# Gate weights loaded ahead of the expert results, their split moved among the last down products, the embedding product in eight steps, and x scaled before it is transposed

## The chip, the cores and the metric

One NeuronCore of a Trainium2 chip runs the whole program. Its engines are TensorE (PE, matrix products, with weight loads PEld), VectorE (DVE), ScalarE (ACT), GpSimd (POOL) and SyncE (SP, which here only issues DMAs); each works through its own instructions in order and they meet through semaphores. 16 DMA engines move data between HBM and the on-chip memories (SBUF, and PSUM for TensorE's results). The metric is device time in microseconds (us) of one launch, the median of the runs shown.

## The reference

Two layers over 512 tokens of width 1024, all in float32. Each layer has an attention part, then a mixture of experts, then a gated embedding ("ple"):

```python
x += (sigmoid(gate_a) * y_a + sigmoid(gate_b) * y_b) @ W_o
x += HierarchicalMoE(RMSNorm(x))     # top-1 of 4 groups, top-2 of 8 experts; 32 experts, hidden 256
x += (p[i] @ W_ple) * sigmoid(RMSNorm(x) @ W_ple_gate)
```

`p[i]` is 512 x 256, `W_ple` 256 x 1024, `W_ple_gate` 1024 x 1024. The change touches the end of the second line and the third.

## The kernel before

**The expert stage.** The 32 experts are worked in 16 pairs, plus one unit (`None`) for an expert that overflowed: 17 units, i = 0 to 16. A unit's rows are fetched by POOL (`fetch`), turned (`turn`, L1134), multiplied by the gate and up weights (`up`, L1151), put through the sigmoid (`act`) and, one round later, multiplied by the down weights (`finish` and `down`, L1163 to L1170); POOL scatters the result to `ybuf` in HBM (L1183). The weights come as 99 loads of 1 MB per layer, all on SP's queue (L1006), chunks 0 to 98 here: a pair takes four for `up` and two for `down`. `Chunks.ahead` issues a load as soon as its SBUF slot (8 KB of every partition) is not among those still to be used. `expert_slots` gives the slots: chunks 0 to 56 go around the 18 of `EXPERT_SLOTS`, the last 42 around the 14 of `LATE_SLOTS`, because slots 5, 10, 11 and 12 are wanted by the embedding. The last unit (i = 16) is special: `finish` of unit 15 runs first, and its chunks are 93 to 96 (`up`) and 97, 98 (`down`); 91 and 92 are the down weights of unit 15.

**The embedding.** In round i = 11 `p` (`praw`) and `W_ple` are loaded on SP's queue; in round 12 `ple_rows` (L1196) transposes `p` and splits it, and in rounds 12 to 15 `ple_product(t)` makes one of the four token tiles of `p @ W_ple`, two halves of 512 columns each.

**The split.** A float32 product that must be exact is made of three faster ones: `split` writes the rounded value on ACT (`hi`, L139 or L142) and the rest on DVE (`lo`, L140 or L143), and `mm3` adds hi·hi, hi·lo and lo·hi (L116 to L118). Weights of a `Stream` are split in pieces; `W_ple_gate` has four column blocks of 256, sources 1 to 4 of `ws2`, each split in 8 pieces, the gain folded in.

**The results and the gate.** When all scatters are done, SP loads `yg[t]`, the two expert results of token tile t, for t = 0 to 3 (L1248), with the gate blocks 1 and 2 behind `yg[0]` and `yg[1]`, and 3 and 4 at the end. `stored(t)` adds the two results to x on DVE (L1258), the last unit's rows come through a product with `which` (L1273, L1276), the sum of squares and its rsqrt `rs` are made on ACT (L1278 to L1281), and `turn_in` (L303) transposes the raw x (L289) and splits it into `gT`. Then the gate product: first half blocks 1 and 2, second half blocks 3 and 4, for four token tiles each (24 TensorE products of 256 columns for a tile and a block). `rs` is applied afterwards: ACT takes |p·r| (L1326), and DVE min(p·r, 0) (L1330). Block 3 is written into block 1's place, and so can be split only when all products with block 1 are done.

**What sets the order.** The Tile framework puts the instructions in a fixed order on each engine when the kernel is built, by program order where an operand is expected to be ready, and fills in later work where it is not. `tc.issue_after` holds an instruction behind another on the same engine.

Of the kernel before, what the change touches and what calls it, by code (L numbers as in the profile page):

```python
# [45 lines left out]
def expert_slots(n):  # L46


    m = n - 3 * len(LATE_SLOTS)
    return [EXPERT_SLOTS[k % len(EXPERT_SLOTS)] if k < m else LATE_SLOTS[(k - m) % len(LATE_SLOTS)] for k in range(n)]  # L50


# [9 lines left out]
def trunk(ctx: ExitStack, tc: tile.TileContext, a, out):  # L62
# [33 lines left out]
    def p_proj():  # L96
        return ps.tile([128, 512], F32, name="proj", tag="proj", bufs=2)
# [204 lines left out]

    def turn_in(xs, hT, t):  # L303
        for h, p in transposed(xs):
            split(p, hT.t[h][:, :, t * 128:(t + 1) * 128])

    class Stream:

# [2 lines left out]
        def __init__(self, srcs, raws, his=(7, 8), pieces=1, first=(), eng=nc.vector, pool=(), depth=None, quick=()):  # L311
            self.pool, self.pooled = pool, None
            self.eng = eng
            self.first = first
            self.srcs, self.raw, self.low, self.done, self.i = srcs, {}, {}, {}, 0
            self.raws, self.his, self.pieces = raws, his, pieces
            self.depth = depth or len(raws)
            self.quick = quick
            self.nsplit = 0

        def load(self, i, eng=nc.sync, parts=1):
            if i < len(self.srcs) and i not in self.raw:
# [15 lines left out]
        def split(self, i, part=None, one=None):  # L338
# [13 lines left out]
            elif i < len(self.srcs) and i not in self.done:  # L352
# [19 lines left out]
                        self.apart(self.hi, lows, self.lo)  # L372
                self.done[i] = w

        def get(self, ahead=1):
            self.i += 1
            for j in range(ahead + 1):
                self.split(self.i - 1 + j)
            return self.done[self.i - 1]
# [16 lines left out]
    for l in range(L):  # L396
        std = (128, KT, 256)
        odd[0] = l % 2 == 1
        ws1 = streams[l]
        ws2 = Stream([(a["wple"][l], (128, 2, D))] + [(a["wpg"][l, c], std, gcol[:, 1]) for c in range(4)], (10, 6, 4, 9), his=(7, 8), pieces=8, first=(5,))  # L400


        if l == 0:
# [753 lines left out]
        def down(u, sg):  # L1157

            n = len_of(u)
            ws = [we.get() for _ in sides(u)]  # L1160
            pt = p_z()
            for c in range(2):
                nc.tensor.transpose(pt[:, c * n:(c + 1) * n], sg[:, c * 128:(c + 1) * 128], ident[:n, :n])  # L1163
            hid = wk.tile([128, 2, 128], F32, name="hid", tag="hid", bufs=2)[:, :, :n]
            nc.scalar.activation(hid, pt[:, :2 * n].rearrange("p (c n) -> p c n", c=2), AF.Copy)  # L1165
            for h in range(2):
                py = p_z()[:n, :]
                for c in range(2):
                    for (_, r), w in zip(sides(u), ws):
                        halves[0] = nc.tensor.matmul(py[r:r + CAP], hid[:, c, r:r + CAP], w[:, c, h * 512:(h + 1) * 512],  # L1170
                                                     start=c == 0, stop=c == 1, tile_position=(0, r),
                                                     skip_group_check=True).ins
                yield py
            we.ahead()
# [11 lines left out]

        pp = [None, None]

        halves, whole = [None], [None]

        def ple_rows():

# [4 lines left out]
                split(p[:, :256].rearrange("p (k n) -> p k n", k=2), pT[:, :, t * 128:(t + 1) * 128])  # L1197
            ws2.get(0)

        def ple_product(t):  # L1200

            wp = ws2.done[0]
            if t % 2 == 0:
                pp[t // 2] = slot(11 + t // 2, [128, 2, D], F32, f"pp{t // 2}")
            for h in range(2):
                p = p_proj()
                with tc.issue_after(halves[0]):
                    whole[0] = mm(p, lambda k: pT[:, k, t * 128:(t + 1) * 128], lambda k: wp[:, k, h * 512:(h + 1) * 512], 2).ins
                nc.scalar.activation(pp[t // 2][:, t % 2, h * 512:(h + 1) * 512], p, AF.Copy)

        last = None
        for i, u in enumerate(units):
            if i + 2 < len(units):
                gs.append(fetch(units[i + 2]))
            if i == len(units) - 6:
                praw = slot(12, [128, NT, 256], F32, "praw")
                nc.sync.dma_start(praw, a["p"][l])
                pT = xgs.tile([128, 2, 2, 512], F32R, name="pT", tag="dhi", bufs=1)
                pT = Pair(pT[:, 0], pT[:, 1])
                ws2.load(0)  # L1220
            if i == len(units) - 5:
                ple_rows()
            if i == len(units) - 1:
                finish(*last)
                break
            if i:
                nxtT = turn(gs[i + 1][0], len_of(units[i + 1]))
            sg = up(u, curT)
            if not i:
                after()  # L1230
                spill[0] = nc.values_load(spi[0:1, 0:1], engines=(mybir.EngineType.SP,), min_val=0, max_val=NE - 1)
                nxtT = turn(gs[1][0], len_of(units[1]))
            if last:
                finish(*last)
            last, curT = (u, sg), nxtT
            if i >= len(units) - 5:
                ple_product(i - len(units) + 5)

        which = wk.tile([128, 512], F32R, name="which", tag="gT", bufs=4)
        tokens = wk.tile([128, 512], F32, name="tokens", tag="gT", bufs=4)  # L1240
# [3 lines left out]
        nc.vector.tensor_scalar(which, tokens, token, None, op0=OP.is_equal)  # L1244
        ygs = []
        for t in range(NT):
            ygs.append(slot(t, [128, 2, D], F32, "yg"))
            nc.sync.dma_start(ygs[t], ybuf.rearrange("(i t p) d -> t p i d", i=2, p=128)[t])  # L1248
            if t < 2:
                ws2.load(t + 1)  # L1250
        ws2.split(1)
        sg = up(u, curT)
        ws2.split(2)

        def stored(t):

# [3 lines left out]
        gT = Halves([15, 16, 17, 18], "gT")  # L1260
        stored(0)
        y = slot(20, [128, 2, D], F32R, "y")
        for h, py in enumerate(down(u, sg)):
            split(py, Pair(y[:, 0, h * 512:(h + 1) * 512], y[:, 1, h * 512:(h + 1) * 512]))
        ws2.load(3)
        ws2.load(4)
        for t in range(NT):
            if t:
                stored(t)
# [9 lines left out]
            r = rs[:, t:t + 1]  # L1279
            nc.scalar.activation(r, ss, AF.Ln, scale=1.0 / D, bias=epsc[:, 0:1])  # L1280
            nc.scalar.activation(r, r, AF.Exp, scale=-0.5)  # L1281
            turn_in(x[:, t], gT, t)
        work2.close()


# [12 lines left out]
        for half in range(2):  # L1298
# [8 lines left out]
            for cc, t in PAIRED:  # L1307
# [12 lines left out]
                    continue  # L1320
                c0, n = (2 * half, 512) if wide else (c, 256)
                p = banks[t] if wide else banks[t][:, cc * 256:(cc + 1) * 256]
                r = rs[:, t:t + 1]
                with tc.high_priority() if not wide else ExitStack():
                    s = wk.tile([128, 512], F32, name="ps", tag="ps", bufs=3)[:, :n]
                    nc.scalar.activation(s, p, AF.Abs, scale=r)  # L1326
                    nc.scalar.activation(s, s, AF.Exp, scale=-1.0)
                    nc.scalar.activation(s, s, AF.Ln, bias=1.0)
                    z = wk.tile([128, 512], F32, name="pz", tag="pz", bufs=3)[:, :n]
                    nc.vector.tensor_scalar(z, p, r, 0.0, op0=OP.mult, op1=OP.min)  # L1330
                    nc.vector.tensor_tensor(s, z, s, op=OP.subtract)
                    nc.scalar.activation(s, s, AF.Exp)
                    cs = slice(c0 * 256, c0 * 256 + n)
                    nc.vector.tensor_tensor(s, s, pp[t // 2][:, t % 2, cs], op=OP.mult)  # L1334
                    nc.vector.tensor_tensor(x[:, t][:, cs], x[:, t][:, cs], s, op=OP.add)  # L1335
# [91 lines left out]
```

## Time and profile before

| | us |
|---|---|
| median of 3 runs | 1549.39 (1548.62 to 1550.88) |
| the profiled execution | 1544.48 |
| its span | 1542.8 |
| PE busy | 1461.7 (95%) |
| DVE busy, ACT busy | 684.4 (44%), 665.6 (43%) |
| mean granted TensorE clock | 0.977 |

The profile is of one execution, in microseconds from the start of its span. Layer 0's expert stage lies between about 440 and 710, layer 1's between about 1200 and 1476; the gate follows each. A busy PE is not a PE at its peak: while it waits for the next piece of a weight, its products follow one another with gaps, and at the lower clock each takes longer.

### The profile page before, as it was taken

Reading aid. Unit: us, or ns where it says so; the run is one execution under the profiler, and the core shown is the slowest. Engines: PE = TensorE matmul, PEld = TensorE weight load, DVE = VectorE, ACT = ScalarE, POOL = GpSimd, SP = SyncE. Lnnn points to the kernel's source line nnn. Section 1 sums busy time; section 2 is a strip of 40 time slices with the busy share of each in tenths; the row PEclk is TensorE's granted clock in tenths of the full one; section 3 lists DMA queues with packets and bytes.
Section 4 is the critical chain, followed back from the end, with each engine's and each line's share of the span. In section 5 each row is a group of like instructions: output and inputs, shape, how many; then the busy total and the mean of one; then the engine's idle time right before and its main releaser. Section 6 shows DMA issues by size and latency. Waiting matters only on the chain. (4 is left out here: it accounts for less than half of the span.)

```text
span 1542.8 us, 21365 instructions
## 1 busy us (share of the span) xinstructions
PE 1461.7 (95%) x8308; PEld 1017.3 (66%) x8308; DVE 684.4 (44%) x1494; ACT 665.6 (43%) x1448; POOL 115.0 (7%) x113
## 2 busy tenths in 40 slices
PE   9999999999989999897999999999999999979886
PEld 7767986888963333335897688778889533324386
DVE  5453565454462111217945526654445422122196
ACT  5664456554322221325846645564533122223266
POOL 0000000000121111010210000000002112110002
PEclk9999999999999999998999999999999999999998
DMA  7200214334479999985131111252262999999731
GB/s 290 104 28 28 106 59 170 100 112 182 162 277 420 418 411 407 421 358 232 56 123 55 55 42 69 83 184 96 76 263 101 354 419 419 399 420 422 316 144 55
DMA packets 60779, 325.43 MB, mean 211 GB/s; under 512 B 11428, under 2 KB 11684, under 8 KB 28032
## 3 DMA queue, kind: packets, MB, share of 16 engines
q1 hardware_dynamic: 50272, 302.10, 49.5%
q0 software_dynamic: 9248, 17.70, 3.1%
q10 hardware_dynamic: 1152, 4.19, 0.7%
q8 instruction: 68, 1.11, 0.3%
q14 instruction: 39, 0.32, 0.1%
HBM read 312.04 MB, written 28.84 MB: 221 GB/s over the span
## 5 line engine op out<-in xcount | busy, mean ns | idle before, releaser
L1151 PE MATMUL proj<-raw,gT 128*64 128x512 f32 x1056 | 259.5, 596 | 1.4 <-DVEq L1077 1.4
L140 DVE TENSOR_TENSOR wlo<-raw,whi 128x1024 fp32r<-128x1024 f32 (+1 forms) x108 | 121.1, 1142 | 135.3 <-ACT whi L139 130.7
L1151 PEld LDWEIGHTS proj<-raw,gT 128*64 128x64 f32 x1056 | 81.3, 137 | 142.3 <-issue 139.9
L1170 PE MATMUL z<-raw,hid 128*64 128x512 f32 x528 | 155.0, 634 | 2.0 <-ACT hid L1165 1.9
L139 ACT ACTIVATE whi<-raw 128x1024 fp32r<-128x1024 f32 (+1 forms) x108 | 104.4, 989 | 89.3 <-PE proj L117 57.9
L802 POOL TENSOR_TENSOR xs<-x,gb 128x512 f32<-128x512 f32 (+2 forms) x34 | 45.6, 1341 | 982.8 <-DVE x L846 819.5
L117 PE MATMUL proj<-wlo,gTh 128*128 128x256 f32 x336 | 97.9, 291 | 4.5 <-DVE wlo L143 4.3
L147 ACT ACTIVATE sgm<-proj 128x256 f32<-128x256 f32 (+1 forms) x34 | 13.0, 383 | 204.2 <-PE proj L1151 204.2
L1170 PEld LDWEIGHTS z<-raw,hid 128*64 128x64 f32 x528 | 45.2, 144 | 82.0 <-issue 72.9
L116 PE MATMUL proj<-whi,gTh 128*128 128x256 f32 x336 | 97.6, 290 | 1.4 <-ACT gTh L139 1.4
L118 PE MATMUL proj<-whi,gTl 128*128 128x256 f32 x336 | 97.2, 289 | 0.0
L1138 DVE COPY gT<-av 128x512 f32<-128x512 f32 (+1 forms) x32 | 21.5, 671 | 149.7 <-PE proj L1151 113.8
L117 PE MATMUL proj<-hTl,whi 128*128 128x512 f32 x192 | 75.6, 394 | 0.0
L117 PE MATMUL proj<-gTl,whi 128*128 128x512 f32 x192 | 75.6, 394 | 0.0
L116 PE MATMUL proj<-gTh,whi 128*128 128x512 f32 x192 | 75.4, 393 | 0.0
L116 PE MATMUL proj<-hTh,whi 128*128 128x512 f32 x192 | 75.4, 393 | 0.0
L118 PE MATMUL proj<-hTh,wlo 128*128 128x512 f32 x192 | 75.4, 392 | 0.0
L118 PE MATMUL proj<-gTh,wlo 128*128 128x512 f32 x192 | 75.3, 392 | 0.0
L116 PE MATMUL proj<-whi,mh 128*128 128x256 f32 x256 | 74.0, 290 | 0.0
L117 PE MATMUL proj<-wlo,mh 128*128 128x256 f32 x256 | 72.9, 285 | 0.0
L118 PE MATMUL proj<-whi,ml 128*128 128x256 f32 x256 | 72.6, 284 | 0.0
L117 PEld LDWEIGHTS proj<-wlo,gTh 128*128 128x128 f32 x336 | 65.9, 196 | 5.9 <-DVE wlo L143 5.9
(341 smaller groups left out, 3287.5 us busy)
## 6 DMA issues: line engine op xcount, KB each, us to landing
raw<-in_wgu_dram SPq DMA_DIRECT2D x132, 1024.0 KB, 19.3
raw<-in_wdn_dram SPq DMA_DIRECT2D x66, 1024.0 KB, 20.0
raw<-in_win_dram SPq DMA_DIRECT2D x37, 1024.0 KB, 4.8
raw<-in_wo_dram SPq DMA_DIRECT2D x8, 1024.0 KB, 4.8
yg<-ybuf SPq DMA_DIRECT2D x8, 1024.0 KB, 11.4
raw<-in_wpg_dram SPq DMA_DIRECT2D x8, 1024.0 KB, 14.9
ybuf<-zero SPq DMA_DIRECT2D x8, 512.0 KB, 5.9
brw<-in_bra_dram SPq DMA_DIRECT2D x16, 256.0 KB, 2.7
```

The lines of the kernel that those rows point to most:

```text
L116: nc.tensor.matmul(o, lhs.hi, rhs.hi, start=start, stop=False, **kw)
L117: nc.tensor.matmul(o, lhs.hi, rhs.lo, start=False, stop=False, **kw)
L118: return nc.tensor.matmul(o, lhs.lo, rhs.hi, start=False, stop=stop, **kw)
L139: r = nc.scalar.activation(dst.hi, src, AF.Copy)
L140: split_lo[0] = eng.tensor_tensor(dst.lo, src, f(dst.hi), op=OP.subtract)
L147: nc.scalar.activation(dst, src, AF.Abs)
L802: nc.gpsimd.tensor_tensor(xs[t][:, cs], x[:, t][:, cs], gb[:, cs], op=OP.mult)
L1138: nc.vector.tensor_copy(gT[h], src)
L1151: nc.tensor.matmul(p[r:r + CAP], gT[h][:, k, r:r + CAP], w[:, k], start=h + k == 0, stop=h + k == 4, tile_position=(0, r), skip_group_chec ...
L1170: halves[0] = nc.tensor.matmul(py[r:r + CAP], hid[:, c, r:r + CAP], w[:, c, h * 512:(h + 1) * 512], start=c == 0, stop=c == 1, tile_positi ...
```

## The change

- `expert_slots`: the last 56 chunks instead of 42 use `LATE_SLOTS`, so the change of rings comes at chunk 43 instead of 57.
- `p` and `W_ple` are loaded in round 7 instead of 11, `ple_rows` is in round 8 instead of 12, and the eight halves of the product are spread over rounds 8 to 15, one each.
- Gate blocks 1 and 2 are issued ahead of `yg[0]`, block 3 ahead of `yg[2]`, block 4 after the turn of tile 1. Places: block 3 in slot 10, block 4 in slot 1 (that of `yg[1]`); block 3's high part goes to slot 9 instead of block 1's place.
- Block 1 is split in `begin` and `piece`: four pieces behind the activation that makes `hid` of the last unit, and ahead of the split of the down product; four pieces behind it. Block 2 follows; block 3 is split behind the last turn.
- x is multiplied by `rs` on ACT (two copies of 512 columns) and then transposed; the sigmoid then works on the plain product, with one DVE instruction less for each tile.

```diff
-    m = n - 3 * len(LATE_SLOTS)
+    m = n - 4 * len(LATE_SLOTS)
...
+        def begin(self, i):
+            self.load(i)
+            self.nsplit += 1
+            shape = list(self.srcs[i][1])
+            self.done[i] = Pair(slot(self.his[(self.nsplit - 1) % len(self.his)], shape, F32R, "whi"), self.low[i])
+        def piece(self, i, c):
+            w, c = self.done[i], slice(c, c + 1)
+            hi = split(self.raw[i][:, c], w[:, c], self.srcs[i][2][:, c])
+            self.apart(hi, self.pieced.setdefault(i, []), split_lo[0])
+            return hi, split_lo[0]
...
-        ws2 = Stream([...], (10, 6, 4, 9), his=(7, 8), pieces=8, first=(5,))
+        ws2 = Stream([...], (10, 6, 4, 10, 1), his=(7, 8, 7, 9, 8), pieces=8, first=(5,))
...
-            if i == len(units) - 6:
+            if i == len(units) - 10:
                 praw = slot(12, [128, NT, 256], F32, "praw")
...
-            if i == len(units) - 5:
+            if i == len(units) - 9:
                 ple_rows()
...
+            k = i - len(units) + 9
+            if k >= 0:
+                ple_product(k // 2, k % 2)
...
         for t in range(NT):
+            ws2.load((1, 3)[t // 2])
+            ws2.load((2, 3)[t // 2])
             ygs.append(slot(t, [128, 2, D], F32, "yg"))
             nc.sync.dma_start(ygs[t], ybuf.rearrange("(i t p) d -> t p i d", i=2, p=128)[t])
-            if t < 2:
-                ws2.load(t + 1)
-        ws2.split(1)
         sg = up(u, curT)
-        ws2.split(2)
...
         for h, py in enumerate(down(u, sg)):
-            split(py, Pair(y[:, 0, h * 512:(h + 1) * 512], y[:, 1, h * 512:(h + 1) * 512]))
-        ws2.load(3)
-        ws2.load(4)
+            if not h:
+                ws2.begin(1)
+                with tc.issue_after(hidden[0].ins):
+                    parts = [ws2.piece(1, c) for c in range(4)][-1]
+            with tc.issue_after(parts[0].ins), tc.issue_after(parts[1].ins):
+                results = split(py, Pair(y[:, 0, h * 512:(h + 1) * 512], y[:, 1, h * 512:(h + 1) * 512]))
+        with tc.issue_after(results.ins), tc.issue_after(split_lo[0].ins):
+            for c in range(4, KT):
+                ws2.piece(1, c)
+        ws2.split(2)
...
-            turn_in(x[:, t], gT, t)
+            for h in range(2):
+                nc.scalar.activation(ygs[t][:, 1, h * 512:(h + 1) * 512], x[:, t][:, h * 512:(h + 1) * 512], AF.Copy,
+                                     scale=r)
+            last_turn = turn_in(ygs[t][:, 1], gT, t)
+            if t == 1:
+                ws2.load(4)
+        with tc.issue_after(last_turn[0].ins), tc.issue_after(last_turn[1].ins):
+            ws2.split(3)
...
-                    nc.scalar.activation(s, p, AF.Abs, scale=r)
-                    nc.scalar.activation(s, s, AF.Exp, scale=-1.0)
-                    nc.scalar.activation(s, s, AF.Ln, bias=1.0)
-                    z = wk.tile([128, 512], F32, name="pz", tag="pz", bufs=3)[:, :n]
-                    nc.vector.tensor_scalar(z, p, r, 0.0, op0=OP.mult, op1=OP.min)
-                    nc.vector.tensor_tensor(s, z, s, op=OP.subtract)
-                    nc.scalar.activation(s, s, AF.Exp)
+                    sigmoid(s, p)
```

## Rows read from the trace of the kernel before

**Rows 1.** The page's row of what the DMA engines moved, in GB/s, in 40 equal slices of the span (38.57 us each).

```profile
GB/s 290 104 28 28 106 59 170 100 112 182 162 277 420 418 411 407 421 358 232 56 123 55 55 42 69 83 184 96 76 263 101 354 419 419 399 420 422 316 144 55
```

**Rows 2.** Busy time by stretch: length, busy us of PE, PEld, DVE, ACT and POOL with instructions, then the granted clock, the DMA share and GB/s. Layer 1's late expert stage, its end, the two halves of its gate; the last row is the second half of layer 0's gate.

```profile
1344.00:1379.00 35.00, 30.50 (x136) 10.92 (x132) 5.96 (x11) 7.27 (x16) 4.04 (x4) 1.00 1.01 411
1379.00:1386.00 7.00, 0.75 (x5) 0.51 (x6) 1.29 (x4) 0.99 (x3) 0.00 (x0) 0.80 1.02 421
1396.00:1456.00 60.00, 57.49 (x245) 23.45 (x244) 8.43 (x16) 13.97 (x30) 4.47 (x5) 1.00 0.88 365
1476.20:1483.00 6.80, 6.80 (x49) 6.75 (x48) 6.80 (x13) 2.64 (x8) 0.00 (x0) 0.81 0.42 172
1483.00:1505.00 22.00, 22.00 (x179) 21.50 (x178) 19.01 (x26) 17.41 (x39) 3.17 (x2) 1.00 0.01 1
1505.00:1531.00 26.00, 24.20 (x192) 23.18 (x191) 21.24 (x38) 20.02 (x45) 5.96 (x4) 1.00 0.11 42
743.50:766.50 23.00, 20.28 (x151) 19.55 (x150) 21.96 (x35) 17.68 (x40) 5.87 (x5) 0.93 0.19 71
```

**Rows 3.** Who waited for whom on PE: from 1345 to 1460 (layer 1), then from 600 to 690 (layer 0). Total us, times, longest.

```profile
PE z L1196 <- DMA praw<-in_p_dram: 6.2, 1, 6.2
...
PE z L1196 <- DMA praw<-in_p_dram: 4.9, 1, 4.9
```

**Rows 4.** SP's issues of single chunks, by time: chunk 43, 96 and 98 of layer 1 (counted back from the last, 98), then 43 and 96 of layer 0.

```profile
1273.77 0.33 SPq L1006 DMA_DIRECT2D raw<-in_wgu_dram  x1
1425.05 0.33 SPq L1006 DMA_DIRECT2D raw<-in_wgu_dram  x1
1430.03 0.33 SPq L1006 DMA_DIRECT2D raw<-in_wdn_dram  x1
...
511.27 0.33 SPq L1006 DMA_DIRECT2D raw<-in_wgu_dram  x1
663.15 0.33 SPq L1006 DMA_DIRECT2D raw<-in_wgu_dram  x1
```

**Rows 5.** us from issue to landing of those loads, each asked for in a stretch that holds it alone: chunk 43 of layer 1, chunk 96 (the same row in both layers), chunk 98 of layer 1, chunk 43 of layer 0; last, from the page, the median of the input weights' loads, of the same size, which have few others beside them.

```profile
raw<-in_wgu_dram SPq DMA_DIRECT2D x1, 1024.0 KB, 21.6
raw<-in_wgu_dram SPq DMA_DIRECT2D x1, 1024.0 KB, 21.0
raw<-in_wdn_dram SPq DMA_DIRECT2D x1, 1024.0 KB, 22.3
raw<-in_wgu_dram SPq DMA_DIRECT2D x1, 1024.0 KB, 22.2
raw<-in_win_dram SPq DMA_DIRECT2D x37, 1024.0 KB, 4.8
```

**Rows 6.** PE by time: the down product of unit 5, whose last operand is chunk 39, in layer 1 and in layer 0; then `up` of the last unit, in layer 1 and in layer 0.

```profile
1294.24 3.65 PE L1170 MATMUL z<-raw,hid 128*64 128x512 f32 x16
...
532.02 3.65 PE L1170 MATMUL z<-raw,hid 128*64 128x512 f32 x16
...
1448.78 7.09 PE L1151 MATMUL proj<-raw,gT 128*64 128x512 f32 x32
...
687.26 7.09 PE L1151 MATMUL proj<-raw,gT 128*64 128x512 f32 x32
```

**Rows 7.** From the chain that ended last, by time: the last two scatters of layer 1, that of unit 14 with chunk loads beside it, that of unit 15 without.

```profile
1443.84 8.32 DMA ybuf<-ring,dst
...
1452.94 3.13 DMA ybuf<-ring,dst
```

**Rows 8.** DVE by time at the end of layer 1's expert stage, from the last unit's result to tile 0 of x; the last row is from the groups by line and shape between 1455 and the end (busy us, mean ns).

```profile
1467.01 0.69 DVE L140 TENSOR_TENSOR y<-z,y 128x512 fp32r<-128x512 f32 x1 [0.49 <-ACT y L139]
1467.62 1.28 DVE L1258 SCALAR_TENSOR_TENSOR x<-yg,gm,x 128x1024 f32<-128x1024 f32 x1
1469.00 0.75 DVE L1276 SCALAR_TENSOR_TENSOR x<-z,gl,x 128x512 f32<-128x512 f32 x1
1469.66 3.25 DVE L143 SCALAR_TENSOR_TENSOR wlo<-raw,gcol,whi 128x256 fp32r<-128x256 f32 x8
1472.83 0.74 DVE L1276 SCALAR_TENSOR_TENSOR x<-z,gl,x 128x512 f32<-128x512 f32 x1
...
L1330 DVE TENSOR_SCALAR pz<-proj,rs 128x512 f32<-128x512 f32 x4 | 3.0, 749 | 1.9 <-ACT ps L1326 1.8
```

**Rows 9.** ACT by time: `hid` and the first half of y of the last unit, and the sum of squares of tile 2 with the end of its `rs`; then the scaled copy of the next norm, from the groups by line and shape.

```profile
1459.84 0.38 ACT L1165 ACTIVATE hid<-z 128x256 f32<-128x256 f32 x1 [1.75 <-PE z L1163]
1464.00 0.60 ACT L139 ACTIVATE y<-z 128x512 fp32r<-128x512 f32 x1 [3.78 <-PE z L1170]
...
1487.05 1.06 ACT L1278 ACTIVATE yg<-x 128x1024 f32<-128x1024 f32 x1
...
1488.90 0.20 ACT L1281 ACTIVATE rs<-rs 128x1 f32<-128x1 f32 x1
...
L1347 ACT ACTIVATE xs<-xs,rs 128x512 f32<-128x512 f32 x4 | 2.9, 720 | 0.3
```

**Rows 10.** PE by time: the product from which layer 1's gate runs without a break, and two neighbours at the full clock.

```profile
1476.25 0.41 PE L118 MATMUL proj<-whi,gTl 128*128 128x256 f32 x1
...
1480.00 0.28 PE L116 MATMUL proj<-whi,gTh 128*128 128x256 f32 x1
1480.12 0.28 PE L117 MATMUL proj<-wlo,gTh 128*128 128x256 f32 x1
```

More of the change, by code (lines that the diff above doesn't have):

```diff
@@ L304, in turn_in @@
         for h, p in transposed(xs):
-            split(p, hT.t[h][:, :, t * 128:(t + 1) * 128])
+            r = split(p, hT.t[h][:, :, t * 128:(t + 1) * 128])
+        return r, split_lo[0]
     class Stream:
@@ L319, in __init__ @@
             self.nsplit = 0
+            self.pieced = {}
         def load(self, i, eng=nc.sync, parts=1):
@@ L399, in trunk @@
         ws1 = streams[l]
-        ws2 = Stream([(a["wple"][l], (128, 2, D))] + [(a["wpg"][l, c], std, gcol[:, 1]) for c in range(4)], (10, 6, 4, 9), his=(7, 8), pieces=8, first=(5,))
+        ws2 = Stream([(a["wple"][l], (128, 2, D))] + [(a["wpg"][l, c], std, gcol[:, 1]) for c in range(4)], (10, 6, 4, 10, 1), his=(7, 8, 7, 9, 8), pieces=8, first=(5,))
         if l == 0:
@@ L1164, in down @@
             hid = wk.tile([128, 2, 128], F32, name="hid", tag="hid", bufs=2)[:, :, :n]
-            nc.scalar.activation(hid, pt[:, :2 * n].rearrange("p (c n) -> p c n", c=2), AF.Copy)
+            hidden[0] = nc.scalar.activation(hid, pt[:, :2 * n].rearrange("p (c n) -> p c n", c=2), AF.Copy)
             for h in range(2):
@@ L1187, in trunk @@
         pp = [None, None]
-        halves, whole = [None], [None]
+        halves, whole, hidden = [None], [None], [None]
         def ple_rows():
@@ L1198, in ple_rows, with ple_product @@
             ws2.get(0)
-        def ple_product(t):
+        def ple_product(t, h):
             wp = ws2.done[0]
-            if t % 2 == 0:
+            if t % 2 == 0 and not h:
                 pp[t // 2] = slot(11 + t // 2, [128, 2, D], F32, f"pp{t // 2}")
[L1205 to L1209, printed above, removed]
+            p = p_proj()
+            with tc.issue_after(halves[0]):
+                whole[0] = mm(p, lambda k: pT[:, k, t * 128:(t + 1) * 128], lambda k: wp[:, k, h * 512:(h + 1) * 512], 2).ins
+            nc.scalar.activation(pp[t // 2][:, t % 2, h * 512:(h + 1) * 512], p, AF.Copy)
         last = None
@@ L1235, in trunk @@
             last, curT = (u, sg), nxtT
-            if i >= len(units) - 5:
-                ple_product(i - len(units) + 5)
+            k = i - len(units) + 9
+            if k >= 0:
+                ple_product(k // 2, k % 2)
         which = wk.tile([128, 512], F32R, name="which", tag="gT", bufs=4)
@@ L1322, in trunk @@
                 p = banks[t] if wide else banks[t][:, cc * 256:(cc + 1) * 256]
-                r = rs[:, t:t + 1]
                 with tc.high_priority() if not wide else ExitStack():
-                    s = wk.tile([128, 512], F32, name="ps", tag="ps", bufs=3)[:, :n]
-                    nc.scalar.activation(s, p, AF.Abs, scale=r)
-                    nc.scalar.activation(s, s, AF.Exp, scale=-1.0)
-                    nc.scalar.activation(s, s, AF.Ln, bias=1.0)
-                    z = wk.tile([128, 512], F32, name="pz", tag="pz", bufs=3)[:, :n]
-                    nc.vector.tensor_scalar(z, p, r, 0.0, op0=OP.mult, op1=OP.min)
-                    nc.vector.tensor_tensor(s, z, s, op=OP.subtract)
-                    nc.scalar.activation(s, s, AF.Exp)
+                    s = wk.tile([128, 512], F32, name="ps", tag="ps", bufs=4)[:, :n]
+                    sigmoid(s, p)
                     cs = slice(c0 * 256, c0 * 256 + n)
```

## The prediction, on record before the change was run

> **What bounds the kernel now.** I first read the 40 slices for where the DMA engines are full: two plateaus near 420 GB/s, the expert stages of the two layers [rows 1]. At that rate 1 MB takes 1.05/0.42 = 2.5 us. Then the stretches: late in layer 1's expert stage PE is busy 57.49 of 60 us beside a DMA share of 0.88 [rows 2], so PE sets that end, and the loads lead by little. Chunk 96 lands at 1425.05 + 21.0 = 1446.05 [rows 4, 5], and the second half of the last `up`, which needs it, begins at 1448.78 + 7.09/2 = 1452.3 [rows 6]: 6.3 us of slack; in layer 0, 684.15 against 690.8, 6.7 us. PE lost its time earlier, waiting for `p`: 6.2 and 4.9 us [rows 3]. Behind the last `up` comes a chain: result, x, transpose, first product. From 1476.25 [rows 10] the first half of the gate is PE's: 22.00 of 22 us busy [rows 2]. In the second half PE waits again, for the split of block 3.
>
> **The part on the rings.** With `LATE_SLOTS` from chunk 43 on, chunk 43 takes slot 3, which chunk 39 held (39 = 2·18 + 3); before, it took slot 12, free since chunk 25. Chunk 39 is the last operand of unit 5's down product, which ends at 1294.24 + 3.65 = 1297.9 in layer 1 and at 535.7 in layer 0 [rows 6]. So chunk 43, issued at 1273.8 now, goes out 24 us later, and all loads of the stage queue behind it. A load with few others beside it lands in 4.8 us [rows 5], so 43 lands at 1302.7 instead of 1273.77 + 21.6 = 1295.4, and at 540.5 instead of 533.5 [rows 4, 5]: 7.3 and 7.0 us. In that hole POOL's fetch and scatter, 0.5 MB each, still move; one of them, 1.25 us, I take off: the loads shift by 6.0 us. Bounds: 4.5 (both moves fall into the hole) to 7.3. The other chunks take slots whose last chunk is 12 or more back.
>
> Chunk 96 then lands at 1452.05 and 690.15, and half an `up`, 3.55, follows: 1455.6 and 693.7 where the last `up` ends now at 1455.87 and 694.35 [rows 6]. **So the end of the stage moves by -0.3 and -0.6 us**; the bounds give -1.8 to +1.0 and -2.1 to +0.7. The wait for `p` (11.1 us over both layers) is not saved: it is replaced by waits for chunks, since the loads have become the later of the two.
>
> The loads of `p` and `W_ple` now stand behind chunks 43 to 52 on SP's queue, so `p` lands some 10.5 · 2.5 = 26 us after 1302.7, about 1329, and in program order `ple_rows` opens round 8, which PE reaches near 1310. Cost zero: from 1329 PE has some 116 us left (eight pairs at 3.65 + 7.09 + 1.3 = 96, the overflow unit 6, transposes of `p` 2, embedding 96 products at 0.13 = 12) and would reach the last `up` before its chunks. The eight halves are the same 96 products as before, on an engine that now waits anyway.
>
> **The part on the gate's loads.** Blocks 1 and 2 no longer wait for the scatters but follow chunk 98, which lands at 1430.03 + 22.3 + 6.0 = 1458.3 [rows 4, 5]: 1460.8 and 1463.3, `yg[0]` 1465.8, `yg[1]` 1468.3. The last scatter, beside loads now, takes 8.3 us instead of 3.1 [rows 7]; it starts near 1450 and is over by 1459, before `yg[0]` could get its turn. Free. Four pieces of block 1 go in front of y's first half: `hid` ends at 1460.2, the pieces take 4 · 3.25/8 = 1.6 us from 1460.8 to 1462.4, and y's first half comes at 1464.0 after 3.78 us of idle ACT [rows 8, 9]. Free, with 1.6 us of margin; a later load costs its lateness.
>
> **The part from the result to the first product.** y's second half is done on DVE at 1467.7 [rows 8]. Now x's tile 0 is whole at 1473.6, with 3.25 us of block 1's split in between; raw halves are transposed as they come, and products run on from 1476.25. After the change DVE has, behind 1467.7: four pieces (1.6), the eight of block 2 (3.25; they stand ahead of the results' loop in the program and their data is there), two L1258 (2.5; `yg[0]` is late, so both), two L1276 (1.4) = 8.8, x whole at 1476.5. Then on ACT, newly in the path: square to `rs`, 1487.05 to 1489.10 now with another instruction between, 1.75 without [rows 9]; the first copy, 0.6 (0.5 to 0.72, the scaled copy of the next norm); transposes 0.5, gTh 0.6, gTl 0.7, as now; handovers 0.25. Sum 4.4: 1480.9. **+4.6 us a layer** (bounds +1.4, block 2 behind x; +5.5, all at the long ends). Layer 0 runs the same instructions. Tiles 1 to 3 hide the same chain: 5.2 us of DVE (2.5 + 1.4 + 1.3) and 4.1 of ACT against 7.2 of PE a tile. The clock: of 1476.2 to 1483 it stood at 0.81 on the mean [rows 2], 6.8 · 0.19 = 1.3 us lost; PE idles longer and I add 0.2 (-0.7 to +1).
>
> **The second half.** 192 products at 0.12 us [rows 10] are 23.0 us; layer 1 takes 26 from 1505 to 1531, layer 0 needs 23.0 for 150 products, which are 18.0 [rows 2]. Block 3, split early, takes the wait away: **-3.0 and -5.0 us** (bounds -1.5 and -3). Block 4 is split while the last tiles of the first half run and is needed 5.8 us into the second. One DVE instruction of 0.75 us less a tile [rows 8] lies beside PE, but for the last tile: -0.2 a layer.
>
> **Sum.** Layer 1: -0.3 + 4.6 + 0.2 - 3.0 - 0.2 = +1.3. Layer 0: -0.6 + 4.6 + 0.2 - 5.0 - 0.2 = -1.0. Together +0.3: a span of 1543.1, a profiled execution of 1544.8. The profiled execution stood 4.9 us under the median of the runs, so the median goes from 1549.4 to about 1550: no change that can be measured.
>
> **Rivals.** (1) Slower: PE, now paced by chunks, falls to 1.2 GHz in the last rounds. The 7 us that hold the wait of 6.2 stood at 0.80, while 4.5 us of idle in 35, in pieces, left it at 1.00 [rows 2, 3]. The price is 3.5 us a layer, half an `up` twice as long behind chunk 96, and any wait for block 1 beyond 1.6 us on top: +7, 1557. It decides once a single wait near the last units is of the size of that for `p`; against it: a pair's loads come in pieces of 2.5 us, and 17.5 us of load against 13.5 of PE a pair leave 4 us in several pieces. The Trainium skill ("TensorE: Matmul & The Clock Gate", "HAM oscillation — how this bites in real kernels") says that waits for loads between short bursts throw the clock back burst after burst; by that rule this rival is the rule and not the exception. The trace agrees for the long wait and not for the short ones. (2) Faster: block 2's split falls behind x's tile 0, since Tile expects its load later than it comes. For it: block 1's split stands behind the first L1276 now [rows 8]. Against: its load is now two places ahead of `yg[0]`. It takes off 3.2 a layer: 1543.5. (3) The ring change costs nothing (fetches fill the hole, or the stage's end was never the loads'): the end comes 2 us earlier a layer, 1546. (4) The early loads are no earlier, since they stand behind late chunks, and y waits for the pieces: +2 a layer, 1554.
>
> **How the numbers follow.** Forecast 0.36, rival 1 0.22, rival 2 0.22, rival 3 0.08, rival 4 0.12. A measurement can tell about 0.2%, 3.1 us. Faster holds rival 2, half of rival 3 and a little of the forecast's spread: 0.30; slower holds rival 1, rival 4 and a little of the spread: 0.34; same 0.36. Most of the chance lies on both sides, so the forecast's own range stands apart: 1547 to 1553. The whole range, 1543.5 to 1557.5, reaches to rivals 1 and 2.
>
> **What would show it.** Chunk 43 of layer 1 issued when unit 5's down product ends, and landing about 5 us later; the wait for `p` gone or moved, waits for chunks in its place; the last `up` ending within 1 us of now. `wlo` of block 2 ahead of L1276, x whole about 9 us behind y, the first lasting run of products 4 to 5 us later against the end of `up`; no wait for `wlo` in the second half. Wrong if PE waits at `ple_rows` and is late at the end, if the clock falls in the last rounds, or if L1276 stands ahead of block 2.

## The result, and the profile after

The changed kernel takes 1566.11 us (median of 1562.76 to 1571.65; before, on the same chip, 1549.01, 1546.2 to 1550.88): a ratio of 1.0122, 95% interval 1.0092 to 1.0151. It is slower by some 17 us and lies above the whole predicted range.

| | before, us | after, us |
|---|---|---|
| the profiled execution | 1544.48 | 1562.76 |
| its span | 1542.8 | 1561.0 |
| PE busy | 1461.7 (95%) | 1459.2 (93%) |
| DVE busy, ACT busy | 684.4, 665.6 | 668.5, 675.3 |
| mean granted TensorE clock | 0.977 | 0.974 |

PE does no more work than before, but waits longer. From the page, the span and what the DMA engines moved, in GB/s, in 40 slices of 39.0 us:

```profile
span 1561.0 us, 21367 instructions
...
GB/s 299 91 29 26 108 82 149 115 88 217 134 323 421 320 420 419 421 396 179 73 110 48 55 55 58 82 192 90 93 270 139 368 418 320 421 419 422 317 98 55
```

Inside each of the two plateaus that were level at 399 to 422 [rows 1] one slice now says 320. One hundred GB/s missing for 39 us are 3.9 MB. Where it falls is seen by stretches of 10 us in layer 1 (length, busy PE, PEld, DVE, ACT and POOL, granted clock, DMA share, GB/s):

```profile
1274.00:1284.00 10.00, 10.00 (x52) 3.74 (x50) 2.56 (x5) 2.83 (x7) 1.96 (x2) 1.00 1.02 417
1284.00:1294.00 10.00, 10.00 (x50) 3.61 (x48) 2.55 (x5) 2.85 (x7) 1.02 (x1) 1.00 0.97 399
1294.00:1304.00 10.00, 10.00 (x53) 3.69 (x50) 1.69 (x4) 2.64 (x7) 2.03 (x2) 1.00 0.38 132
1304.00:1314.00 10.00, 10.00 (x48) 3.64 (x46) 0.69 (x1) 0.98 (x2) 2.02 (x2) 1.00 0.88 334
```

The hole ends when chunk 43 goes out, and that is when unit 5's down product ends. PE by time, unit 5's down product and the last `up`, in layer 1 and in layer 0 (before: [rows 6]):

```profile
1300.36 3.65 PE L1186 MATMUL z<-raw,hid 128*64 128x512 f32 x16
...
1465.59 7.09 PE L1167 MATMUL proj<-raw,gT 128*64 128x512 f32 x32
...
532.64 3.65 PE L1186 MATMUL z<-raw,hid 128*64 128x512 f32 x16
...
693.62 7.09 PE L1167 MATMUL proj<-raw,gT 128*64 128x512 f32 x32
```

SP's issues of chunk 43 in the two layers (before: [rows 4]), and of `p` in layer 1:

```profile
1304.06 0.33 SPq L1022 DMA_DIRECT2D raw<-in_wgu_dram  x1
...
536.34 0.33 SPq L1022 DMA_DIRECT2D raw<-in_wgu_dram  x1
...
1315.66 0.33 SPq L1232 DMA_DIRECT2D praw<-in_p_dram  x1
```

PE's waits for `p` (before: [rows 3]), layer 0, then layer 1, with its waits for `sgm` (the result of the sigmoid) up to the last `up`, and PE's first product on `p`; then SP's issues of chunk 96 in layer 1 and layer 0 (before: [rows 4]):

```profile
PE z L1212 <- DMA praw<-in_p_dram: 10.7, 1, 10.7
...
PE z L1212 <- DMA praw<-in_p_dram: 10.8, 1, 10.8
PE z L1179 <- DVE sgm L1088: 8.6, 5, 1.8
...
1338.78 1.97 PE L1212 MATMUL z<-ident,praw 128*128 128x128 f32 x8 [10.83 <-DMA praw<-in_p_dram]
...
1438.76 0.33 SPq L1022 DMA_DIRECT2D raw<-in_wgu_dram  x1
...
669.73 0.33 SPq L1022 DMA_DIRECT2D raw<-in_wgu_dram  x1
```

From the end of unit 5's down product to the end of the last `up`, layer 1 took 157.98 us [rows 6] and now takes 1472.68 - 1304.01 = 168.7; layer 0 took 158.7 and takes 164.4. **So the expert stages lost 10.7 and 5.7 us.** The rest by stretch: the stretch with the wait for `p` and the last 60 us of the stage in layer 1, the two halves of its gate, and the second half of layer 0's gate (before: [rows 2]):

```profile
1330.00:1345.00 15.00, 5.75 (x20) 3.04 (x22) 4.06 (x6) 3.80 (x7) 0.00 (x0) 0.54 1.02 420
1412.00:1472.00 60.00, 54.97 (x226) 20.78 (x226) 8.43 (x16) 12.02 (x25) 5.47 (x6) 1.00 0.90 376
1498.00:1525.80 27.80, 27.80 (x226) 27.38 (x225) 17.49 (x29) 21.26 (x46) 1.30 (x1) 1.00 0.11 39
1525.80:1549.00 23.20, 23.10 (x193) 22.90 (x191) 17.11 (x29) 19.23 (x45) 6.89 (x5) 1.00 0.12 47
754.60:777.60 23.00, 21.77 (x183) 21.52 (x182) 18.92 (x34) 20.57 (x48) 7.47 (x6) 1.00 0.26 93
```

From the last `up` to the first lasting product of the gate: 20.4 us before, now 1498.03 - 1472.68 = 25.4 in layer 1, and 26.2 against 20.6 in layer 0: **+5.0 and +5.6**. The first half of the gate is 0.9 and 1.0 shorter, the second 2.9 in layer 1 (25.95 to 23.03) and 5.8 in layer 0 with what follows it, up to layer 1's first products. The sums are about +12 and +4.5, and some 1.6 lie elsewhere: together the 18.2 by which the spans differ. DVE, then ACT, on the chain behind the last down product of layer 1 (before: [rows 8, 9]):

```profile
1482.86 0.69 DVE L140 TENSOR_TENSOR y<-z,y 128x512 fp32r<-128x512 f32 x1 [1.90 <-ACT y L139]
1483.46 3.25 DVE L143 SCALAR_TENSOR_TENSOR wlo<-raw,gcol,whi 128x256 fp32r<-128x256 f32 x8
...
1490.60 1.40 DVE L1298 SCALAR_TENSOR_TENSOR x<-z,gl,x 128x512 f32<-128x512 f32 x2
...
1492.04 1.06 ACT L1300 ACTIVATE yg<-x 128x1024 f32<-128x1024 f32 x1 [4.43 <-DVE x L1298]
...
1493.78 1.33 ACT L1305 ACTIVATE yg<-x,rs 128x512 f32<-128x512 f32 x2
1495.71 0.60 ACT L139 ACTIVATE gTh<-z 128x512 fp32r<-128x512 f32 x1 [0.59 <-PE z L289]
```

Twelve pieces of split stand between y and x's tile 0 (eight in the second row, four among the `yg` additions), as many as the prediction had, and x is whole 8.4 us behind y's last piece.

### The profile page after: what moved, and what is told of

Same layout as the page of the kernel before. It is cut to its first block, busy times and chain, and to the rows that moved or that the text cites. A ratio compares the mean times of both kernels' runs of the same rounds, so it can differ in the third digit from the quotient of the medians.

```text
span 1561.0 us, 21367 instructions
## 1 busy us (share of the span) xinstructions
PE 1459.2 (93%) x8308; PEld 1012.0 (65%) x8308; DVE 668.5 (43%) x1476; ACT 675.3 (43%) x1464; POOL 113.1 (7%) x113
## 5 line engine op out<-in xcount | busy, mean ns | idle before, releaser
L1167 PE MATMUL proj<-raw,gT 128*64 128x512 f32 x1056 | 254.5, 596 | 1.7 <-DVEq L1093 1.7
L116 PEld LDWEIGHTS proj<-whi,gTh 128*128 128x128 f32 x336 | 64.6, 192 | 0.8 <-issue 0.6
## 6 DMA issues: line engine op xcount, KB each, us to landing
raw<-in_wgu_dram SPq DMA_DIRECT2D x132, 1024.0 KB, 20.4
```

Source lines behind the costliest of these rows:

```text
L116: nc.tensor.matmul(o, lhs.hi, rhs.hi, start=start, stop=False, **kw)
L1167: nc.tensor.matmul(p[r:r + CAP], gT[h][:, k, r:r + CAP], w[:, k], start=h + k == 0, stop=h + k == 4, tile_position=(0, r), skip_group_chec ...
```

## The experiments

Five theories. A: the early embedding puts `p` behind a burst of ten chunks, and `ple_rows` keeps its place on PE. B: the rings as such (starved loads) cost. C: the longer chain from the result to the first product costs. D, formed after the second group: the hole in the loads at chunk 43, which one slot makes, is all of the rings' cost. E, formed with it: PE's order in the rounds, which the framework fixes when the kernel is built, takes time that the waits hide. Ratios are to the kernel before.

**1. The tail alone** (`e_tail_only`) and **2. the stage alone** (`e_stage_only`).

```diff
 # e_tail_only: the changed kernel with
-    m = n - 4 * len(LATE_SLOTS)
+    m = n - 3 * len(LATE_SLOTS)
...
-            if i == len(units) - 10:
+            if i == len(units) - 6:
...
-            if i == len(units) - 9:
+            if i == len(units) - 5:
...
-            k = i - len(units) + 9
+            k = i - len(units) + 5
             if k >= 0:
-                ple_product(k // 2, k % 2)
+                ple_product(k, 0)
+                ple_product(k, 1)
 # e_stage_only: the kernel before with the changed kernel's lines at these places
```

> The changed kernel with the stage of the kernel before: rings from chunk 57 on, p and W_ple loaded in the sixth round from the end, p transposed in the fifth, both halves of a tile's products in one round. Only the part from the last up on is changed. Theory A (the loss is PE's wait for p, which the early embedding makes): near the kernel before, 1546 to 1552; from the changed kernel's trace the tail gives +5.0 - 0.9 - 2.9 in layer 1 and +5.6 - 1.0 - 5.8 in layer 0, with +0.2 at the end, +0.2 in all; PE waits for p as before, about 5 and 6 us. Theory C (the loss is the longer chain from the result to the first product): 1560 or more. Theory B (the rings alone): near the kernel before too.

> The kernel before with the changed stage alone: four rings of late slots, p and W_ple loaded three rounds earlier, p transposed in front of eight rounds that take half a tile's product each. Theories A and B: slower by the whole loss, 1562 to 1568, with a wait for p of 10 to 11 us in each layer by A, and by B with waits for chunks. Theory C: near the kernel before, 1547 to 1552.

Measured: the tail 1548.78, ratio 1.0003 (0.9992 to 1.0014); the stage 1567.01, 1.0121 (1.0100 to 1.0142). All of the loss is the stage's, the tail is neutral: C falls.

**3. `p` earlier** (`e_p_early`), and **4. with block 2's split behind x's tile 0** (`e_both`).

```diff
-            if i == len(units) - 10:
+            if i == len(units) - 11:
 # e_both in addition:
-        ws2.split(2)
...
+                merged = nc.vector.scalar_tensor_tensor(xc, p, gl[:, t:t + 1], xc, op0=OP.mult, op1=OP.add)
+            if not t:
+                with tc.issue_after(merged.ins):
+                    ws2.split(2)
```

> The changed kernel with the loads of p and W_ple one round earlier, so that SP issues them ahead of chunk 43 and not behind chunk 52; p is still transposed where it was. Theory A: the waits of 10.7 and 10.8 us go, with the low clock behind them (about 2 and 3 us), and no wait for chunks takes their place: 1538 to 1546. Theory B (the starved loads of the rings are the cost): the wait for p turns into waits for chunks, 1558 to 1566. Theory C: 1560 or more.

> As the kernel with the loads of p and W_ple one round earlier, and in addition block 2 of the gate is split behind tile 0's x instead of ahead of it. If the step from the result to the first product is set by VectorE's order, as the forecast has it: x of tile 0 is whole some 3 us earlier in each layer, 3 to 7 us off the kernel with the early loads, 1533 to 1541. If the order of that split is beside the path (PE or ScalarE sets the first product, or block 2 then comes too late): within 2 us of it.

Measured: 1552.32, 1.0030 (1.0012 to 1.0048); with the later split 1548.23, 1.0007 (0.9989 to 1.0025). The waits for `p` are gone and 14 us came back, fewer than the 20 to 28 that A gave. No wait for chunks came. PE in layer 1, 1290 to 1480:

```profile
PE z L1179 <- DVE sgm L1088: 13.7, 7, 3.3
```

The waits for `sgm` grew in place of `p`'s (before, 9.0 in 5; in both kernels 3.3 of it are behind the last `up`). This made me doubt A. The later split shortened PE's wait for the first scaled x from 10.5 to 7.6 us a layer, and the median by 4.

**5. The rings alone** (`e_ring_only`), **6. `p` used later** (`e_rows_late`), **7. `p` earlier without the rings** (`e_tail_p`), **8. the same with block 2 later** (`e_tail_p_b2`).

```diff
 # e_ring_only: the kernel before with
-    m = n - 3 * len(LATE_SLOTS)
+    m = n - 4 * len(LATE_SLOTS)
 # e_rows_late: the changed kernel with
-            if i == len(units) - 9:
+            if i == len(units) - 7:
                 ple_rows()
...
-            k = i - len(units) + 9
-            if k >= 0:
-                ple_product(k // 2, k % 2)
+            k = i - len(units) + 7
+            for h in ((0, 1), (2, 3), (4,), (5,), (6,), (7,))[k] if k >= 0 else ():
+                ple_product(h // 2, h % 2)
 # e_tail_p: e_tail_only with p and W_ple loaded at len(units) - 8 instead of - 6
 # e_tail_p_b2: e_tail_p with the later split of block 2
```

> The kernel before with four rings of late slots instead of three, and nothing else; p and the embedding stay where they were. The stage alone cost 18 to 19 us, and with p loaded ahead of chunk 43 some 4 us were left. Theory A (all of the loss is the early embedding, whose p stands behind the burst of chunks): near the kernel before, 1545 to 1551, with waits for p of 5 to 7 us. Theory B in its smaller form (the starved loads, or the order of PE that is planned on them, cost what was left): slower by 3 to 8 us, 1551 to 1556.

> The changed kernel with p and W_ple loaded where it has them, behind chunk 52, but p transposed two rounds later and the eight halves of products spread over six rounds (two, two, one, one, one, one). Theory A says that only the distance from the load of p to its use counts: the wait of 10.7 us goes as it did with the earlier load, 1548 to 1556. If the early place of the load itself was what helped (its 1.5 MB out of the burst), the wait turns into waits for chunks: 1558 or more.

> The kernel with the stage of before and the changed tail, with the loads of p and W_ple two rounds earlier; p is transposed where it was. If PE's waits for p (about 5 and 6 us) and the low clock behind them are on the path to the last up, as they were in the changed kernel: 8 to 13 us off the time of the kernel with the tail alone, 1536 to 1541; more than the slack of the chunks (6.3 and 6.7 us) can't come in a layer. If the loads or the order of PE set that end: 1545 to 1550.

> The same with block 2 of the gate split behind tile 0's x. The step took some 4 us off beside the kernel with the early p. If the parts add up: 1531 to 1537, faster than both kernels; if the second half of the gate or the loads take it back: as the kernel without that step.

Measured: rings alone 1561.95, 1.0087 (1.0059 to 1.0116); `p` used later 1568.12, 1.0120 (1.0095 to 1.0145); `p` earlier without the rings 1551.09, 1.0016 (1.0003 to 1.0030); with block 2 later 1550.93, 1.0020 (1.0005 to 1.0035). A missed three times, and B, in the smaller form it had by then (1551 to 1556), once. The rings alone make most of the loss; a use of `p` two rounds later gains nothing; and in the old rings an earlier `p` gains nothing either. The later split took 2.9 us off the same wait here too (10.5 to 7.6), and the median didn't move: its worth isn't settled.

The hole in the kernel with the rings alone, in stretches of 10 us up to and past chunk 43's issue; then PE's waits in layer 1, of the rings alone and of `p` used later:

```profile
1277.90:1287.90 10.00, 10.00 (x52) 3.70 (x50) 2.56 (x5) 2.82 (x7) 1.96 (x2) 1.00 1.02 417
1287.90:1297.90 10.00, 10.00 (x50) 3.60 (x48) 2.56 (x5) 2.85 (x7) 1.04 (x2) 1.00 0.94 389
1297.90:1307.90 10.00, 10.00 (x53) 3.69 (x50) 1.69 (x4) 2.64 (x7) 1.99 (x2) 1.00 0.34 118
1307.90:1317.90 10.00, 10.00 (x46) 3.80 (x46) 0.69 (x1) 0.98 (x2) 2.02 (x2) 1.00 0.90 324
```

```profile
PE z L1163 <- DVE sgm L1072: 8.0, 5, 3.3
PE z L1196 <- DMA praw<-in_p_dram: 6.2, 1, 6.2
PE proj L1151 <- DMA raw<-in_wgu_dram: 4.7, 6, 1.4
```

```profile
PE z L1179 <- DVE sgm L1088: 11.7, 7, 1.8
PE proj L1167 <- DMA raw<-in_wgu_dram: 5.0, 1, 5.0
```

Against a level 420 GB/s the four stretches lack 3 + 31 + 302 + 96 GB/s, which over 10 us each are 4.3 MB or 10.3 us of load. Behind the hole the loads stay late: against the end of unit 5's down product `p` lands 7.2 us (layer 1) and 5.8 us (layer 0) later than in the kernel before. With the rings alone PE waits 4.7 us for chunks on the way to `p` and then 6.2 us for `p`, as before; with `p` used later it waits 5.0 us for a chunk. That suggests D.

Why an earlier `p` gained nothing without the rings is on PE: its waits in layer 1 with `p` where it was (`e_tail_only`), then with `p` earlier (`e_tail_p`), and a round of the latter by time:

```profile
PE z L1179 <- DVE sgm L1088: 9.1, 5, 3.3
PE z L1212 <- DMA praw<-in_p_dram: 6.0, 1, 6.0
```

```profile
PE z L1179 <- DVE sgm L1088: 13.5, 7, 3.3
PE z L1212 <- DVE pT L140: 1.6, 1, 1.6
```

```profile
1385.08 3.22 PE L1167 MATMUL proj<-raw,gT 128*64 128x512 f32 x13
1387.71 0.59 PE L1186 MATMUL z<-raw,hid 128*64 128x512 f32 x1
1388.13 0.59 PE L1167 MATMUL proj<-raw,gT 128*64 128x512 f32 x1
1388.14 1.45 PE L1186 MATMUL z<-raw,hid 128*64 128x512 f32 x3
1389.52 0.66 PE L1150 MATMUL av<-ident,ring 128*128 128x128 f32 x4
1391.92 0.33 PE L1179 MATMUL z<-ident,sgm 128*128 128x128 f32 x1 [1.74 <-DVE sgm L1088]
```

`up` is hardly over when the transposes of its own `sgm` stand next in PE's order, with the rest of the previous unit's down product behind them: PE stops 1.74 us for the sigmoid. The down product has also begun with one side of its pair alone. Products of two sides that stand in turn start together (16 in 3.65 us in [rows 6], 0.43 us from pair to pair); a product alone takes such a slot for itself, and the records of the stage (`up` and down products from unit 5's down product to the last `up`) show 267 slots where `e_tail_only` has 259: 8 · 0.43 = 3.4 us. With 4.4 more of waits for `sgm` and the 1.6 for `pT` that is 9.4, more than the 6.0 of `p` and what the clock gave back. That suggests E.

**9. The rings without chunk 43** (`e_ring_but43`), **10. the changed kernel with chunk 43 in slot 5** (`e_slot5`), **11. the mended order** (`e_tail_p_order`), **12. both** (`e_slot5_order`).

```diff
 # e_ring_but43: e_ring_only with slots[m] = 12;  e_slot5: the changed kernel with
-    return [EXPERT_SLOTS[k % len(EXPERT_SLOTS)] if k < m else LATE_SLOTS[(k - m) % len(LATE_SLOTS)] for k in range(n)]
+    slots = [EXPERT_SLOTS[k % len(EXPERT_SLOTS)] if k < m else LATE_SLOTS[(k - m) % len(LATE_SLOTS)] for k in range(n)]
+    slots[m] = 5
+    return slots
 # the mended order, in down():
+            with tc.issue_after(halves[0]) if halves[0] else ExitStack():
                 for c in range(2):
                     nc.tensor.transpose(pt[:, c * n:(c + 1) * n], sg[:, c * 128:(c + 1) * 128], ident[:n, :n])
+            before_it = None
...
+                        with tc.issue_after(before_it) if before_it else ExitStack():
                             halves[0] = nc.tensor.matmul(py[r:r + CAP], hid[:, c, r:r + CAP], w[:, c, h * 512:(h + 1) * 512],
                                                          start=c == 0, stop=c == 1, tile_position=(0, r),
                                                          skip_group_check=True).ins
+                        before_it = halves[0]
```

> The kernel before with four rings of late slots, but chunk 43 kept in slot 12; all the other chunks of the new ring are where the four rings put them. The four rings alone cost 13 us at a ratio of 1.0087; their trace shows the DMA engines at 119 GB/s for the 10 us before chunk 43 may go out, and PE waiting for chunks (4.5 and 4.7 us). Theory D (the hole that chunk 43 makes by waiting for chunk 39's slot is the cost of the rings): the whole loss goes, 1545 to 1550, no hole in the slices. Theory E (the order of PE, planned on the rings, is the cost, and the rings as such change it): 1555 or more.

> The changed kernel with one number changed: chunk 43 goes into slot 5, whose last chunk is 30, instead of slot 3. Theory D: the hole goes, chunks and p come some 10 us earlier against unit 5's down product, the wait for p shrinks from 10.8 us to 3 or less: 1545 to 1553. Theory A (p behind the burst of ten chunks, whatever the hole): the wait for p stays at 8 us or more, 1558 to 1566.

> The kernel with the stage of before, the changed tail and p two rounds earlier, with PE's order mended in the rounds: the two sides of a down product alternate, and a unit's transposes of sgm stand behind the previous unit's down product. Without it, taking PE's wait for p away gained nothing: PE waited 13.5 us for sgm (7 times) where it had waited 9.0 (5 times), and had 267 slots of matmuls where it had 259. Theory E (that order is where the gain went): 4 to 6 us a layer off the kernel without it, 1539 to 1545, with waits for sgm of 5 us or less. If the loads set the end: within 2 us of it, and waits for chunks in place of the waits for sgm.

> The changed kernel with chunk 43 in slot 5 and the mended order of PE. If D and E both hold and add up: 1537 to 1545, faster than both kernels. If the loads are the bound once PE's order is mended: 1545 to 1550, with waits for chunks.

Measured: the rings without chunk 43 1548.16, 0.9992 (0.9979 to 1.0005); the changed kernel with slot 5 1550.27, 1.0015 (0.9999 to 1.0030); the mended order 1538.47, 0.9933 (0.9909 to 0.9957); both 1540.24, 0.9946 (0.9926 to 0.9965). **D holds twice**: one slot of 99 is the rings' whole cost, and 16 of the 17 us of the change. The changed kernel with slot 5 around the same place (unit 5's down product ends at 1301.16), and its wait for `p`:

```profile
1281.00:1291.00 10.00, 10.00 (x52) 3.72 (x50) 2.55 (x5) 2.83 (x7) 1.02 (x1) 1.00 1.02 420
1291.00:1301.00 10.00, 10.00 (x53) 3.56 (x50) 1.69 (x4) 2.61 (x7) 2.03 (x2) 1.00 1.02 418
1301.00:1311.00 10.00, 10.00 (x46) 3.75 (x45) 0.69 (x1) 0.98 (x2) 2.02 (x2) 1.00 1.02 419
```

```profile
PE z L1214 <- DMA praw<-in_p_dram: 2.9, 1, 2.9
```

`p` stands behind chunk 52 in this kernel too. Only the hole is gone, and with it 8 us of the wait. **E holds** as well, the median half a microsecond beyond its range: with the mended order PE waits for `sgm` only behind the last `up`, small waits for chunks appear, and the stage takes 153.8 and 153.0 us where `e_tail_p` took 158.0 and 159.7. Its two edits were not tried apart. The slots went from 267 to 264 and 265 only, while all of PE's waits in the stage went from 13.3 us to 9.5 and 8.6, so here most of the gain is in the waits:

```profile
PE z L1180 <- DVE sgm L1088: 3.3, 1, 3.3
...
PE proj L1167 <- DMA raw<-in_wgu_dram: 2.8, 3, 1.0
```

**13. The changed kernel with the mended order and the hole** (`e_after_order`), **14. the kernel before with the mended order** (`e_before_order`), **15. all together** (`e_best`: slot 5, the order, `p` one round earlier, block 2 later). The edits are those above.

> The changed kernel with its rings as they are (chunk 43 in slot 3) and the mended order of PE. Theory D (a hole of about 4 MB in a stage whose loads fill the DMA engines to its end moves that end by its length, some 10 us a layer less what slack there was): 1552 to 1562, with the wait for p still near 10 us or waits for chunks in its place. Theory E (the hole cost only through the order of PE): 1538 to 1546, as the kernel with slot 5 and the mended order.

> The kernel before with the mended order of PE alone. If the loss by the order was there before the change: 3 to 5 us a layer off, 1538 to 1543, with waits for sgm of 4 us or less instead of 9; the wait for p (4.9 and 6.2 us) then grows by what PE comes earlier, so it may be less. If the order only costs where p no longer holds PE up: 1545 to 1549.

> The changed kernel with chunk 43 in slot 5, the mended order, the loads of p and W_ple one round earlier and block 2 split behind tile 0's x. Each took its part in other runs (16, 10, 1 to 3 for what is left of the wait for p, and 4 us): 1532 to 1538 if the stage is PE's to its end, 1538 to 1541 if the loads set it once PE's order is mended.

Measured: 1558.41, 1.0071 (1.0050 to 1.0092); 1539.56, 0.9945 (0.9925 to 0.9965); 1537.79, 0.9936 (0.9921 to 0.9950). With the mended order the hole costs 1558.41 - 1540.24 = 18 us in the two layers, as much as with the old one, so it needs no help from E. PE's wait for `p` in layer 1 is as in the changed kernel:

```profile
PE z L1216 <- DMA praw<-in_p_dram: 10.7, 1, 10.7
```

The order was no fault of the change: the kernel before gains 9 us by it, as expected, though its wait for `p` (6.5 in layer 1) is no shorter. The last kernel is faster than both (about 11 us before, 28 after), but its interval overlaps that of the kernel before with the mended order. It came in just inside the range that took the stage to be PE's to its end, yet its trace shows the other case: the second half of the last `up` starts when chunk 96 lands, in both layers (layer 1 here). With the order mended, the loads set the end:

```profile
1443.74 3.65 PE L1169 MATMUL proj<-raw,gT 128*64 128x512 f32 x14 [1.39 <-DMA raw<-in_wgu_dram]
```

What beats both kernels is the order; that the change itself adds anything to it isn't shown.

## Why the prediction was wrong, step by step

- **The hole was seen, and its shift of the loads was about right.** That chunk 43 would wait for unit 5's down product was right to 0.1 us (1304.01 and 1304.06). The shift was taken as 6.0 us. Measured from the end of unit 5's down product, chunk 96 goes out after 134.8 us where it took 127.2 (layer 1), and after 133.4 where it took 127.5 (layer 0): a shift of 7.6 and 6.0 us. Counted in what was not moved, the four stretches of layer 1 lack 3 + 21 + 288 + 86 GB/s, 4.0 MB, 9.5 us. The two differ in part because the kernel before had a small hole at its own change of rings, where chunks 59 to 63 take slots used 8 to 10 loads before: 41 GB/s lack for 15 us, some 1.5 us of load, and in the changed kernel that is gone (419 to 420 there). Layer 1 before:

```profile
1330.00:1345.00 15.00, 14.44 (x60) 4.84 (x56) 2.55 (x5) 3.62 (x8) 2.58 (x3) 1.00 0.98 379
```

- **The step that failed: `ple_rows` at "cost zero".** The prediction itself had `p` landing some 19 us after PE would reach it, and let that cost nothing because PE had "some 116 us left" and would still be at the last `up` before its chunks. By its numbers `p` lands 31 us after unit 5's down product and PE is through 116 later, 147 in all, ten short of the 157.7 that it gave the loads. Measured in layer 1: 34.8 and 133.9, together 168.7. Of the 21.6 us between, 18 are in the 116 (133.2 were measured with slot 5 too) and 3.7 in the landing of `p`. The 116 were work alone; left out were the waits for `sgm` (8.6), products that go singly, and the half clock (0.50 for the 5.9 us behind the wait and again for 3.4 near 1390, some 4.7 us lost). So PE, not the loads, set the end: chunk 96 went out at 1438.76 and, at the 20.5 to 24.2 us that it took in the runs that show its landing, was there by 1459 to 1463 (an estimate), while PE began the half that needs it at 1469.1. A late `p` is then paid. The prediction had named this sign itself ("Wrong if PE waits at `ple_rows` and is late at the end").
- **"The loads have become the later of the two" was asked at one point only.** The 6 us of slack were read at chunk 96. Loads and PE also meet at `p`, and there the kernel before had no slack at all: the 6.2 and 4.9 us [rows 3] were the loads being late. That the wait for `p` "is replaced by waits for chunks" came true only where `p` was used later (5.0 us). In the changed kernel the wait for `p` grew by 4.6 us (layer 1) and 5.8 (layer 0). In layer 0 that is as much as the 5.7 us by which the stage's end moved, instead of -0.6. In layer 1 the half clock behind `p` cost about 2.6 us more than before and 5 more slots of products some 2 us; with the 4.6 that is some 9 of the 10.7 us, instead of -0.3.
- **Result to first product: right, in part by luck.** +4.6 forecast, +5.0 and +5.6 measured, by the chain named, with block 2 ahead of x. But from x to the first lasting product it took 6.0 us instead of 4.4, and y came 1.0 us earlier against the end of `up`: the sum is nearer than its parts. The clock term of +0.2 came out the other way: the first half of the gate got 0.9 and 1.0 shorter, outside the -0.7 that bounded it, and began at a granted clock of 1.00. **The second half: right.** -3.0 and -5.0 forecast with -0.2 beside each, -2.9 and -5.8 measured. **The gate's loads: free**, as forecast. The tail alone at 1.0003 agrees with the sum of these, which was +1.6 in layer 1 and -0.4 in layer 0.
- **The rivals.** Rival 1 had the right sign and a wrong place: no wait for chunks and no low clock in the last rounds (1.00 over the last 60 us), but the wait for `p` 130 us earlier, with a mean of 0.54 over 15 us. The rule of the Trainium skill beside it ("TensorE: Matmul & The Clock Gate", "HAM oscillation — how this bites in real kernels") agrees with the trace for that wait, as it did before; the waits in the page's own case are longer than the short ones here, so these are no test of it. The three waits of 1.6 to 1.8 us in the last 60 us left the clock at 1.00, though one of the two such waits before them stands beside a dip (0.92 from 1390 to 1405). Rival 2's split, made in experiment 4, is worth 2.9 us of wait a layer, as near as the 3.2 claimed for it. Rivals 3 and 4 didn't come.

Why `p` one round earlier took back 14 us although the hole, smaller by the 1.5 MB of `p` and `W_ple`, was still there, fits the same reading. In that kernel chunk 96 went out at 1428.62, 130.9 us behind unit 5's down product (129.5 in layer 0): a shift of 3.7 and 2.0 us, less than the slack of 6.3 and 6.7. PE waited for no chunk, and the stage took 160.1 and 157.8 us where it took 158.0 and 158.7 before. The hole costs where PE meets a load without slack, and `p` behind it was that load. What stays open: how much each of the two edits of the order is worth, and whether a smaller hole costs anything once the order is mended.

## What to carry to other kernels

Where a change delays a load in a stage that keeps the DMA engines full, ask at every place where an engine meets a load, small ones in the same queue too, whether there is slack; a wait that is there already says there is none. Before a late load is let cost nothing because an engine has time left, take that time from the trace with its waits and its clock, not from the work alone. In a ring of buffers look at the seam: one slot that was used four loads ago made a hole of 4 MB, and one number took it out. When a wait is taken away and the time stays, compare the engine's order before and after: an order fixed at build time can hold waits of its own that the first wait had hidden.

## What the runs showed of the hardware

A load of 1 MB took about 21 to 22 us from issue to landing in the full queue and 4.8 with few others beside it [rows 5]; chunk 43 behind the hole took 5.2 and 6.6 (the rings alone, layers 0 and 1). Products of 64 columns on the two halves of the array started in pairs, 0.43 us from pair to pair, where they stood in turn in PE's order; a product alone took the same 0.43 us. A wait of 10.8 us left PE at a mean granted clock of 0.54 over 15 us, while three waits of 1.6 to 1.8 us in the last 60 us of the stage left it at 1.00, and one of 1.7 us stands beside 3.4 us at 0.5.
